# Two down projections of the layer-0 sample-side FFN as seven block products, with their weight sums made in DRAM earlier

## The chip, the cores and the metric

The kernel runs on one core of a Trainium2 chip. The core has a matrix engine (TensorE, PE in the profile; its weight loads are shown as PEld), a vector engine (VectorE, DVE), an engine for activations (ScalarE, ACT), GpSimd (POOL) and a queue engine (SyncE, SP). The first four work in order, each on its own instructions, and wait for each other and for transfers by semaphores. SP issues most of the transfers from DRAM; POOL issues those that add to what lies at the destination, and gathers. The metric is the device time of one execution in microseconds (us).

## The reference

One inference step of a decoder with two layers, width 1024, for a prompt of 1024 tokens and 8 sample tokens that share the weights, in fp32. In every layer a mixer (a gated recurrence in layer 0, stick-breaking attention in layer 1) runs beside a cross-attention into 256 memory tokens, and then comes the SwiGLU FFN, which is what the change touches:

```python
D_MODEL = 1024
D_FF = ((8 * D_MODEL + 3 * 256 - 1) // (3 * 256)) * 256

def swiglu(h, w_gu, w_down):
    gate, up = jnp.split(h @ w_gu, 2, axis=-1)
    return (jax.nn.silu(gate) * up) @ w_down
```

D_FF is 2816, which is 22 slices of 128 rows. The output of the down projection has 8 blocks of 128 columns, `m` = 0 to 7.

## The kernel before

**Tiling.** Activations lie transposed, with features on the 128 partitions and tokens along the free dimension. The tokens are split into two halves, called groups: `g = 0` has 512 prompt columns, `g = 1` has the other 512 and the 8 sample tokens, 520 columns, worked as two pieces of 260. A product in fp32 is made as three products of a faster format: a weight tile is split into a high part (a copy on ScalarE) and a rest (a subtraction on VectorE), an activation likewise, and high × high, high × rest and rest × high are added up in PSUM. `split_w` (L253) loads and splits weights, `proj` (L280) makes a projection with them, and `evac_raw` (L476) adds its result to the running output `R` in SBUF.

**FFN in steps.** The 22 slices are worked in five steps, `PARTS = [(0, 5), (5, 5), (10, 4), (14, 4), (18, 4)]` (first slice, slices). A step makes its gate and up slices, `silu(gate) * up` gives as many tiles `m`, and its down projection adds their product with the weights to `R`. Class `ffn` does this with `proj` for both groups of layer 0 (`f0`, `f1`) and for the first group of layer 1. A down step of four slices and 520 columns is 8 output blocks × 4 slices × 3 products × 2 pieces = 192 matmuls of 260 columns.

**The block form, in layer 1.** The second group of layer 1 is done by class `ffn_w`. Its steps 1, 2 and 3 have a down projection in another form, `down_w`. The weights of a step are seen as 2 × 2 blocks of 2 slices by 512 columns, the activations as 2 × 2 blocks of 2 slices by 260 columns, and the product is made of seven block products in place of eight, as Strassen's form does it. For this, four sums of weight blocks (`s1` to `s4`) are needed, and three sums of activation blocks (`ys`, made at the end of the gate and up slices). A product is 12 matmuls for each pair of output blocks; a step is 2 pairs × 7 products × 12 = 168 matmuls. The products are `product(q, j)`: `q` is one of four running sums in PSUM of which each is added to or subtracted from `R` at set points by `add` (L769, VectorE, 128 × 260), and copied with its sign turned by `minus` (L773, ScalarE). The pairs `acc[i][q]`, `i` = 0 and 1, take all eight PSUM banks, one tile of the pool "quads" for each.

**Weight sums.** They are made in DRAM, out of the weights themselves, by `summed` (L653 to L672): eight transfers for each step, four of them accumulating, each issued by POOL. So that a transfer starts at a chosen place of the program, each has a marker ahead of it: ScalarE copies one column of a tile just made (`after()`, L666; three buffers `rr`), POOL copies that (L667; one buffer `mk`), and the transfer stands behind it in POOL's order (L670 accumulating, L672 plain). `down_sums` makes them for the down weights of a layer (`dsum`, 512 KB for each transfer), `weight_sums` for the gate and up weights of layer 1 (`wsum`, 1 to 1.25 MB, five steps of eight transfers).

**The order of work.** Each part of the model is a generator, and `weave((a, na), (b, nb), ...)` runs several of them together, `na` and `nb` being how many pieces each has. What comes out is a program that a scheduler then puts into order on each engine, by its own estimate of when operands come; so weight loads and splits stand well ahead of their matmuls, and matmuls of the next projection are at times put between others. Buffers limit that: five raw weight tiles `w`, five split ones `ws`, eight tiles `a`, four tiles `c`, seven tiles `b`; in PSUM two tiles `mm` of two banks each, three of one bank `s` and one `ns`.

The stages around the change, in order: layer-0 memory attention of the first half, `a0.mem`, beside the second half's projections `a1.fq`; the output projection `o0.mm`; `o0.finish` beside `a1.v` and `a1.qm`; then layer 0's FFN for the first half; and, much later, `f1`, the second half's FFN: its steps 0 and 1 beside layer 1's attention `b0` and its steps 2, 3, 4, with `ws`, the weight sums of layer 1, beside both.

Of the kernel before, what the change touches and what calls it, by code (L numbers as in the profile page):

```python
# [9 lines left out]
F32 = mybir.dt.float32  # L10
# [8 lines left out]
P = 128  # L19
# [5 lines left out]
def tile_decoder(  # L25
# [229 lines left out]

    def split_w(W, k0, nk, m0):
        out = []
        for a in range(0, nk, 4):
            n = min(4, nk - a)
            raw = wraw.tile([P, 4, P], F32, tag="w", name=nm("w"))  # L260
            nc.sync.dma_start(
                raw[:, :n, :],
                W[(k0 + a) * P : (k0 + a + n) * P, m0 : m0 + P].rearrange("(k p) m -> p k m", p=P),
            )
            ws = wspl.tile([P, 2, 4, P], F32R, tag="ws", name=nm("ws"))
            nc.scalar.copy(ws[:, 0, :n, :], raw[:, :n, :])  # L266
            nc.vector.tensor_sub(ws[:, 1, :n, :], raw[:, :n, :], ws[:, 0, :n, :].bitcast(F32))  # L267
            for i in range(n):
                out.append((ws[:, 0, i, :], ws[:, 1, i, :]))
        return out  # L270
# [281 lines left out]

    def gate_up_w(l, f, ops, spl, raws, pair=None):
# [52 lines left out]
        mt = M(F32R)  # L606

        def put_sum(dst, d, a, b):
            nc.vector.tensor_sub(d, a, b)
            split_to((dst[:, 0], dst[:, 1]), d)  # L610

        if not pair:
            w = n if pair is None else h
            split_to((mt[:, 0, :w], mt[:, 1, :w]), sg[:, :w])
            if pair is not None:
                put_sum(mt[:, :, h:n], sg[:, :h], sg[:, h:n], sg[:, :h])
                pair.append((mt, sg))
            return mt
        m0, s0 = pair.pop()
        split_to((mt[:, 0, :n], mt[:, 1, :n]), sg[:, :n])  # L620
        y = [bpool.tile([P, 2, h], F32R, tag="b", name=nm("ys")) for _ in range(3)]
        put_sum(y[2], s0[:, h:n], s0[:, h:n], sg[:, h:n])
        put_sum(y[1], sg[:, h:n], sg[:, h:n], s0[:, :h])
        put_sum(y[0], sg[:, :h], sg[:, :h], sg[:, h:n])
        pair.extend((m0[:, :, :h], mt[:, :, :h], mt[:, :, h:n], y[0], m0[:, :, h:n], y[1], y[2]))
        return mt
# [48 lines left out]
    dsums = {}  # L675
    htok = []
# [3 lines left out]
    class ffn_w:  # L680
# [47 lines left out]
        def down_w(self, pi, f0, pairs, extra):  # L728
            l, n, h, R = self.l, NG[1], PW[1], self.R
            a11, a12, a21, a22 = down_blocks(l, f0)  # L730
            s1, s2, s3, s4 = dsums[pi]
            src = ((a11, 0), (s1, 4), (s2, 5), (a12, 1), (s3, 6), (s4, 2), (a22, 3))
            for m0 in (0, 2):
                ms = (m0, m0 + 1)
                acc = [[Q(i) for i in range(4)] for _ in ms]

                def weight(rows):
                    r = self.raws().rearrange("p k m -> p (k m)")
                    nc.sync.dma_start(r.rearrange("p (t c) -> p t c", t=2), rows[:, :, m0 * P : (m0 + 2) * P])
                    w = self.spl()  # L740
                    split_to((w[:, 0, :], w[:, 1, :]), r)
                    return w

                def slice_of(q, hf, a, first=False):
                    for i in range(2):
                        o = hf * 256 + i * P
                        for wi, (wj, xi) in enumerate(((0, 0), (0, 1), (1, 0))):
                            nc.tensor.matmul(
                                acc[i][q][:, :h], we[:, wj, o : o + P], extra[0][:, xi, a * h : (a + 1) * h],
                                start=(first and wi == 0), stop=(wi == 2), skip_group_check=True,  # L750
                            )

                def product(q, j, first=False):
                    w = weight(src[j][0])
                    for i in range(2):
                        for t in range(2):
                            x = pairs[t][src[j][1]]
                            o = t * 256 + i * P
                            for wi, (wj, xi) in enumerate(((0, 0), (0, 1), (1, 0))):
                                nc.tensor.matmul(  # L760
                                    acc[i][q][:, :h], w[:, wj, o : o + P], x[:, xi, :],
                                    start=(first and t == 0 and wi == 0), stop=(t == 1 and wi == 2),
                                    skip_group_check=True,
                                )

                def add(q, mo, a, sub=False):
                    for i, m in enumerate(ms):
                        d = R[m + mo][:, a * h : (a + 1) * h]
                        (nc.vector.tensor_sub if sub else nc.vector.tensor_add)(d, d, acc[i][q][:, :h])  # L769

                def minus(q, p):
                    for i in range(2):
                        nc.scalar.activation(acc[i][q][:, :h], acc[i][p][:, :h], AF.Copy, scale=-1.0)  # L773

                product(0, 0, True)
                minus(1, 0)
                product(3, 1, True)
                product(1, 2)
                minus(2, 1)
                product(0, 3)  # L780
                if extra:
                    tail = w_down[l][(f0 + 4) * P : (f0 + 5) * P, :].rearrange("p (o m) -> p o m", o=2)
                    we = weight(tail)
                    slice_of(0, 0, 0)
                add(3, 4, 1)
                add(0, 0, 0)
                product(1, 4)
                add(3, 0, 1, True)
                add(1, 4, 1)
                product(2, 5)  # L790
                if extra:
                    slice_of(2, 0, 1)
                add(2, 0, 1)
                product(1, 6)
                if extra:
                    slice_of(1, 1, 0)
                    slice_of(0, 1, 1, True)
                    add(0, 4, 1)
                add(1, 4, 0)
                yield  # L800

        def down(self, pi):
# [9 lines left out]
            if self.block(pi):  # L812
                yield from self.down_w(pi, f0, pairs, mids[4:])
# [29 lines left out]
    class ffn:  # L843
        def __init__(self, g, l, xt, rows=False):
            self.g, self.l, self.xt, self.rows = g, l, xt, rows
            self.R = self.acc = None

        def part(self, pi):
            g, l = self.g, self.l
# [3 lines left out]
            mids = []  # L853
            for j in range(nf):
                pg = proj(g, w_gu[l], 0, ND, (f0 + j) * P, self.xt)
                sg = silu(None, pg, g)
                pu = proj(g, w_gu[l], 0, ND, DFF + (f0 + j) * P, self.xt)
# [932 lines left out]
```

## Time and profile before

| | |
|---|---|
| runs, median | 2445.47 us (2444.11 to 2445.83, 3 runs) |
| the profiled execution | 2445.71 us |
| its span, by the profile | 2443.6 us, mean granted TensorE clock 0.998 |
| around the span | 2.1 us |
| `f1` steps 0 and 1, beside the attention | 990 to 1206.8 us |
| `f1` steps 2 to 4 | 1206.8 to 1411.3 us |
| in these, down projection of step 2 | 1250.3 to 1273.4 us |
| down projection of step 3 | 1319.3 to 1342.3 us |
| `a0.mem` with `a1.fq`, `o0.mm` | 229 to 335 us |
| the block form in layer 1, steps 2 and 3 | 2290.4 to 2310.5 and 2350.9 to 2371.0 us |

In a row of grouped instructions stand the line, the engine, the operation, output and inputs by the program's names without their numbers, and the tile; behind it the busy time and the mean of one. In a row of the timeline the first number is the start in us from the span's start and the second the length. The table of stages gives for each engine the busy time with the number of instructions, then the granted TensorE clock (1.00 is full), the mean busy share of the 16 transfer engines and their GB/s. A row of waits has the waiting engine, line and operand, what ended the wait, and then the total, how often, and the longest. In a row of the page's part on transfers the last number is the time from issue to landing.

### The profile page before, as it was taken

What the parts mean: (1) busy time and instruction counts of PE and PEld (TensorE: products, weight loads), DVE (VectorE), ACT (ScalarE), POOL (GpSimd) and SP (SyncE); (2) the same over time, 40 slices, a digit from 0 to 9 for tenths busy, and PEclk for the clock granted to TensorE, in tenths of its full rate; (3) what the DMA queues carried; (4) which work ended last, traced back from release to release, by engine and by line L of the source; (5) the groups of instructions that cost most, each with busy time, mean ns of one, the idle gap of its engine ahead of it and who ended that gap; (6) DMA issues with size and microseconds to landing.
All of it is one profiled execution on the core that took longest, in us unless ns stands there. A gap on an engine that the chain in (4) does not pass through costs nothing.

```text
span 2443.6 us, 40814 instructions
## 1 busy us (share of the span) xinstructions
PE 2403.0 (98%) x15401; PEld 2131.2 (87%) x15401; DVE 1598.5 (65%) x2785; ACT 1229.1 (50%) x2438; POOL 132.5 (5%) x201
## 2 busy tenths in 40 slices
PE   7999999999999999999999999999999999999997
PEld 6888988888877887999999989877787797999997
DVE  5777556765775576555544485777678648757885
ACT  4547544444444454555433454555454445565664
POOL 2000001200000000010111100022000000000000
PEclk9999999999999999999999999999999999999999
DMA  5353255774543446456688876544454234366651
GB/s 177 101 159 109 71 162 132 183 201 132 177 138 94 133 153 212 119 136 152 168 207 205 246 181 199 159 141 147 124 151 134 87 118 125 124 192 175 185 168 66
DMA packets 499224, 369.24 MB, mean 151 GB/s; under 512 B 19758, under 2 KB 444315, under 8 KB 499027
## 3 DMA queue, kind: packets, MB, share of 16 engines
q1 hardware_dynamic: 476114, 307.91, 42.3%
q0 software_dynamic: 22912, 58.73, 10.4%
q8 instruction: 121, 1.98, 0.3%
q14 instruction: 77, 0.62, 0.1%
HBM read 336.74 MB, written 80.15 MB: 171 GB/s over the span
## 4 chain that ended last, share of the span: by engine, by line
PE 89%; DVE 4%; DMA 2%; ACT 2%; issue 1%; SPq 0%; POOL 0%; DVEq 0%; ACTq 0%; POOLq 0%
PE mm L280 61%; PE q L581 7%; PE q L760 2%; PE q L822 2%; PE q L539 2%; PE mm L1208 2%; PE s L1058 1%; PE s L1017 1%; PE s L1391 1%; PE mm L994 1%; PE s L1566 1%; PE mm L967 1%; DMA b<-qd 1%; PE s L1605 1%; DVE ws L267 1%
## 5 line engine op out<-in xcount | busy, mean ns | idle before, releaser
L280 PE MATMUL mm<-x,ws 128*128 128x260 f32 (+1 forms) x7776 | 1329.7, 330 | 0.0
L280 PEld LDWEIGHTS mm<-x,ws 128*128 128x128 f32 x7776 | 1148.2, 188 | 143.4 <-issue 8.6
L266 ACT CAST ws<-w 128x512 fp32r<-128x512 f32 (+1 forms) x680 | 402.6, 593 | 653.1 <-PE mm L280 558.0
L267 DVE TENSOR_TENSOR ws<-w,ws 128x512 fp32r<-128x512 f32 (+1 forms) x680 | 443.4, 655 | 242.9 <-ACT ws L266 237.7
L280 PE MATMUL mm<-m,ws 128*128 128x512 f32 (+1 forms) x2112 | 392.1, 342 | 0.2 <-DVE r L476 0.2
L280 PEld LDWEIGHTS mm<-m,ws 128*128 128x128 f32 x2112 | 323.3, 188 | 47.0 <-issue 3.2
L572 DVE TENSOR_TENSOR ws<-w,ws 128x512 fp32r<-128x512 f32 x126 | 86.6, 691 | 46.4 <-ACT ws L571 43.5
L581 PE MATMUL q<-y,ws 128*128 128x260 f32 x864 | 112.7, 283 | 0.0
L581 PEld LDWEIGHTS q<-y,ws 128*128 128x128 f32 x864 | 107.3, 188 | 0.0
L476 DVE TENSOR_TENSOR r<-r,mm 128x512 f32<-128x512 f32 (+1 forms) x96 | 66.0, 688 | 57.1 <-PE mm L280 56.0
L571 ACT CAST ws<-w 128x512 fp32r<-128x512 f32 x126 | 77.8, 618 | 47.2 <-PE q L581 15.2
L320 DVE TENSOR_SCALAR t<-mm 128x512 f32<-128x512 f32 (+1 forms) x74 | 51.2, 691 | 64.3 <-PE mm L280 64.1
L858 DVE TENSOR_TENSOR t<-t,mm 128x512 f32<-128x512 f32 (+1 forms) x66 | 45.5, 689 | 67.9 <-PE mm L280 67.5
L324 DVE TENSOR_TENSOR t<-t,t 128x512 f32<-128x512 f32 (+1 forms) x66 | 45.8, 694 | 65.7 <-ACT t L323 65.7
L581 PE MATMUL q<-x,ws 128*128 128x260 f32 x648 | 86.9, 283 | 0.0
L581 PEld LDWEIGHTS q<-x,ws 128*128 128x128 f32 x648 | 81.7, 189 | 0.0
L343 DVE TENSOR_TENSOR st<-st,n 128x512 f32<-128x512 f32 (+1 forms) x98 | 67.1, 691 | 8.1 <-ACT n L342 6.6
L667 POOL COPY mk<-rr 128x1 f32<-128x1 f32 x64 | 29.3, 458 | 751.3 <-ACT rr L666 751.3
L321 ACT ACTIVATE t<-t 128x512 f32<-128x512 f32 (+1 forms) x66 | 41.9, 635 | 40.7 <-DVE t L320 36.3
L287 ACT CAST m<-t 128x512 fp32r<-128x512 f32 (+1 forms) x76 | 47.4, 623 | 25.3 <-DVE t L858 18.0
L822 PE MATMUL q<-m,ws 128*128 128x260 f32 x432 | 53.6, 284 | 0.0
L288 DVE TENSOR_TENSOR m<-t,m 128x512 fp32r<-128x512 f32 (+1 forms) x76 | 52.5, 691 | 1.2
(379 smaller groups left out, 2811.8 us busy)
## 6 DMA issues: line engine op xcount, KB each, us to landing
w<-in_w_gu SPq DMA_DIRECT2D x334, 256.0 KB, 3.2
w<-in_w_down SPq DMA_DIRECT2D x156, 256.0 KB, 3.0
w<-in_w_in_a SPq DMA_DIRECT2D x80, 256.0 KB, 3.0
wsum<-in_w_gu POOLq DMA_DIRECT2D x18, 1024.0 KB, 9.1
w<-wsum SPq DMA_DIRECT2D x72, 256.0 KB, 3.6
w<-in_w_o SPq DMA_DIRECT2D x64, 256.0 KB, 2.9
dsum<-in_w_down POOLq DMA_DIRECT2D x18, 512.0 KB, 6.5
w<-in_w_mem_kv SPq DMA_DIRECT2D x32, 256.0 KB, 3.2
```

The source lines that it names most:

```text
L266: nc.scalar.copy(ws[:, 0, :n, :], raw[:, :n, :])
L267: nc.vector.tensor_sub(ws[:, 1, :n, :], raw[:, :n, :], ws[:, 0, :n, :].bitcast(F32))
L280: nc.tensor.matmul(ps[:, a, : PW[g]], wt, xt[k][:, xi, o : o + PW[g]], start=(k == 0 and wi == 0), stop=(k == nk - 1 and wi == 2),)
L288: nc.vector.tensor_sub(dst[1], src, dst[0].bitcast(F32))
L320: nc.vector.tensor_scalar(sv(x, g), pv(ps, g), -44.0, None, op0=ALU.max)
L343: nc.vector.tensor_add(acc[:, :n], acc[:, :n], t[:, :n])
L476: nc.vector.tensor_add(dst, dst, pv(ps, g))
L539: nc.tensor.matmul(pp[a][:, :h], wt, xt[k][:, xi, a * h : (a + 1) * h], start=(k == 0 and wi == 0), stop=(k == ND - 1 and wi == 2),)
L571: nc.scalar.copy(w[:, 0, :], src)
L572: nc.vector.tensor_sub(w[:, 1, :], src, w[:, 0, :].bitcast(F32))
L581: nc.tensor.matmul(ps[:, :h], w[:, wj, k * P : (k + 1) * P], x[:, xi, :], start=(first and k == 0 and wi == 0), stop=(k == 3 and wi == 2), ...
L822: nc.tensor.matmul(pp[a][:, :h], wt, mids[k][:, xi, a * h : (a + 1) * h], start=(k == 0 and wi == 0), stop=(k == nf - 1 and wi == 2),)
```

## The change

The down projections of steps 2 and 3 of `f1` (layer 0, second group) use the block form. `down_w` becomes a function of its own that gets its PSUM tiles, buffers and a hook from the caller; it now yields twice for each pair of output blocks. The function `paired`, which makes the activation sums, is taken out of `gate_up_w`, so that `ffn` can use it. In `ffn` the four running sums of a pair have other PSUM tiles: `q = 0` and `q = 3` a bank each (`s`, or `ns` for the last), `q = 1` and `q = 2` the two banks of one `mm` tile. The steps' order becomes: gate and up of step 2, the first slice of step 3, down of step 2, the rest of step 3, the first slice of step 4, down of step 3, the rest of step 4, its down.

The weight sums of these two steps are 16 transfers, put beside `a0.mem` with `a1.fq` (7), `o0.mm` (5) and `o0.finish` with `a1.v` and `a1.qm` (4); their markers read a split weight tile (`now`). Of the 40 steps of layer 1's weight sums, 21 in place of 16 now stand beside the attention and 19 in place of 24 beside steps 2 to 4.

```diff
+            now[0] = ws[:, 0, 0, 0:1].bitcast(F32)
...
+    def paired(sg, pair):
...
-            dsums[i] = t
+            dsums[l, i] = t
...
+    def down_w(l, pi, R, pairs, extra, raws, spl, banks, each):
...
+            acc = [banks(i) for i in range(2)]
...
+            add(0, 0, 0)
+            yield
+            product(1, 4)
+            add(3, 0, 1, True)
+            add(1, 4, 1)
+            product(2, 5)
...
+            add(2, 0, 1)
+            product(1, 6)
...
+            add(1, 4, 0)
+            each(ms)
+            yield
...
+        def spl(self):
+            self.n += 1
+            if self.n % 8 in (1, 4, 6):
+                return cpool.tile([P, 2, 512], F32R, tag="c", name=nm("ws"))
+            return wspl.tile([P, 2, 512], F32R, tag="ws", name=nm("ws"))
+
+        def raws(self):
+            self.r += 1
+            if self.r % 2:
+                if not self.half:
+                    t = apool.tile([P, 2, 4, P], F32, tag="a", name=nm("w"))
+                    self.half = [t[:, 0], t[:, 1]]
+                return self.half.pop(0)
+            return wraw.tile([P, 4, P], F32, tag="w", name=nm("w"))
...
+                sg = silu(N() if block else None, pg, g)
...
+                if block:
+                    mids.append(paired(sg, pairs[j // 2]))
...
+                def four(i):
+                    two = mmp.tile([P, 2, 512], F32, tag="mm", name=nm("mm"))
+                    return [S(), two[:, 0, :], two[:, 1, :], NS() if i else S()]
...
+                yield from down_w(l, pi, self.R, pairs, mids[4:], self.raws, self.spl, four, each)
+                return
...
-    weave((a0.mem(), 8), (a1.fq(), 8))
+    ds = down_sums(0, (2, 3), lambda: now[0])
+    weave((a0.mem(), 8), (a1.fq(), 8), (islice(ds, 7), 8))
     o0 = out_proj(0, 0, M)
-    drain(o0.mm(a0.xo))
-    weave((o0.finish(), 17), (chain(a1.v(), a1.qm(A)), 8))
+    weave((o0.mm(a0.xo), 8), (islice(ds, 5), 5))
+    weave((o0.finish(), 17), (chain(a1.v(), a1.qm(A)), 8), (ds, 4))
...
-    f1 = ffn(1, 0, o1.x)
+    f1 = ffn(1, 0, o1.x, (2, 3))
     ws = weight_sums(1, range(5), lambda: f1.now, 4)
-    weave((chain(b0.sb(), b0.mem()), 24), (chain(f1.part(0), f1.part(1)), 18), (islice(ws, 16), 17))
-    weave((chain(f1.part(2), f1.part(3), f1.part(4)), 24), (ws, 24))
+    weave((chain(b0.sb(), b0.mem()), 24), (chain(f1.part(0), f1.part(1)), 18), (islice(ws, 21), 22))
+    lagged = chain(
+        f1.gate_up(2), f1.gate_up(3, 0, 1), f1.down(2), f1.gate_up(3, 1), f1.gate_up(4, 0, 1), f1.down(3),
+        f1.gate_up(4, 1), f1.down(4),
+    )
+    weave((lagged, 24), (ws, 19))
```

On TensorE, at the down projection of step 2, an output block stood before as a run over the four slices `m`, three products and two pieces each, in one `mm` tile; the next block follows with the other tile:

```order
L280 MATMUL mm_12366<-m_11947,ws_12363 128x260 x6
L280 MATMUL mm_12366<-m_12085,ws_12363 128x260 x6
L280 MATMUL mm_12366<-m_12219,ws_12363 128x260 x6
L280 MATMUL mm_12366<-m_12353,ws_12363 128x260 x6
L280 MATMUL mm_12397<-m_11947,ws_12394 128x260 x6
L280 MATMUL mm_12397<-m_12085,ws_12394 128x260 x6
```

Now, in the first pair of output blocks of that step, the rows from the end of product(1, 2) on read as follows. `mm_12640` and `mm_12643` hold q1 and q2 of `i` = 0 and 1, `s_12790` is q0 of the next pair, and rows of `m_12201` with `mm` are product(1, 4), of `ys_12204` product(2, 5):

```order
L715 MATMUL mm_12643<-ys_12489,ws_12728 128x260 x3
L715 MATMUL s_12790<-m_12064,ws_12797 128x260
L715 MATMUL mm_12640<-m_12201,ws_12749 128x260 x3
L715 MATMUL mm_12640<-m_12484,ws_12749 128x260 x3
L715 MATMUL s_12790<-m_12064,ws_12797 128x260 x2
L715 MATMUL mm_12643<-m_12201,ws_12749 128x260 x3
L715 MATMUL mm_12643<-m_12484,ws_12749 128x260 x3
L715 MATMUL s_12790<-m_12347,ws_12797 128x260 x2
L715 MATMUL mm_12640<-ys_12204,ws_12767 128x260 x3
L715 MATMUL mm_12640<-ys_12487,ws_12767 128x260 x3
```

Single matmuls of the next pair's product(0, 0) have moved between the products of the first pair. In the second pair of each step the products stand one behind the other.

On VectorE, in the second pair of step 2, the sums (L724) stand between weight splits (L269) of the gate and up weights that come next. The first row is an add of q3, then come those of q0 (`s`), and those of q1 and q2 (`mm`):

```order
L724 TENSOR_TENSOR r_10159<-r_10159,ns_12794 128x260 x2
L269 TENSOR_TENSOR ws_12946<-w_12944,ws_12946 128x512
L724 TENSOR_TENSOR r_10159<-r_10159,s_12790 128x260
L269 TENSOR_TENSOR ws_13007<-w_13005,ws_13007 128x512
L724 TENSOR_TENSOR r_10159<-r_10159,s_12793 128x260
L269 TENSOR_TENSOR ws_13012<-w_13010,ws_13012 128x512
L724 TENSOR_TENSOR r_10159<-r_10159,mm_12789 128x260
L724 TENSOR_TENSOR r_10159<-r_10159,mm_12792 128x260
L724 TENSOR_TENSOR r_10159<-r_10159,mm_12789 128x260
L724 TENSOR_TENSOR r_10159<-r_10159,mm_12792 128x260
L269 TENSOR_TENSOR ws_13082<-w_13080,ws_13082 128x512
L724 TENSOR_TENSOR r_10159<-r_10159,mm_12789 128x260
```

Where before one sum of 520 columns followed each output block, six sums of 260 columns for each `i` now follow the products of a pair.

More of the change, by code (lines that the diff above doesn't have):

```diff
@@ L605, in gate_up_w @@
         nc.vector.tensor_mul(sg[:, h:n], sg[:, h:n], gt[:, h:n])
[L606 to L626, printed above, removed]
+        return paired(sg, pair)
     sums = {}
@@ L726, in gate_up @@
                 yield
[L728 to L800, printed above, removed]
@@ L812, in down @@
             if self.block(pi):
-                yield from self.down_w(pi, f0, pairs, mids[4:])
+                yield from down_w(
+                    l, pi, self.R, pairs, mids[4:], self.raws, self.spl, lambda i: [Q(q) for q in range(4)], lambda ms: None
+                )
                 return
@@ L852, in part @@
             last = pi == len(PARTS) - 1
[L853 to L857, printed above, removed]
-                nc.vector.tensor_mul(sv(sg, g), sv(sg, g), pv(pu, g))
-                mt = M(F32R)
-                split_to((mt[:, 0, :n], mt[:, 1, :n]), sg[:, :n])
-                mids.append(mt)
-                self.now = sg[:, 0:1]
-                yield
+            mids, pairs = self.mids.pop(pi)
             if pi == 0:
```

110 lines of the change are left out of this document (102 added, 8 removed).

## The prediction

> **What bounds the kernel now.** I read the page's busy times first, then its chain of waits, then a table of busy time by stage, and last the rows of single engines inside the stages that the change touches.
>
> ```profile
> span 2443.6 us, 40814 instructions
> PE 2403.0 (98%) x15401; PEld 2131.2 (87%) x15401; DVE 1598.5 (65%) x2785; ACT 1229.1 (50%) x2438; POOL 132.5 (5%) x201
> PE 89%; DVE 4%; DMA 2%; ACT 2%; issue 1%; SPq 0%; POOL 0%; DVEq 0%; ACTq 0%; POOLq 0%
> PE mm L280 61%; PE q L581 7%; PE q L760 2%; PE q L822 2%; PE q L539 2%; PE mm L1208 2%; PE s L1058 1%; PE s L1017 1%; PE s L1391 1%; PE mm L994 1%; PE s L1566 1%; PE mm L967 1%; DMA b<-qd 1%; PE s L1605 1%; DVE ws L267 1%
> ```
>
> TensorE is busy for 98% of the span and carries 89% of the chain, 61% of it by the plain projections of L280. A matmul taken out therefore shortens the kernel by its own time, unless TensorE then waits. The stages, in order of time (before the layer-0 second half; its steps 0 and 1 beside attention; its steps 2 to 4; layer 1's two block downs), read:
>
> ```profile
> core 0: us, PE busy (x) PEld busy (x) DVE busy (x) ACT busy (x) POOL busy (x), PEclk, DMA share, GB/s
> 1250.30:1273.40 23.10, 23.10 (x195) 23.10 (x194) 11.64 (x17) 6.27 (x13) 4.21 (x7) 1.00 0.90 214
> 1206.80:1411.30 204.50, 204.50 (x1709) 204.46 (x1708) 101.92 (x149) 82.31 (x150) 31.33 (x47) 1.00 0.83 213
> 2290.40:2310.50 20.10, 20.10 (x170) 20.10 (x169) 18.54 (x42) 11.90 (x24) 0.00 (x0) 1.00 0.66 187
> 2350.90:2371.00 20.10, 20.10 (x171) 20.10 (x170) 18.32 (x41) 11.73 (x23) 0.00 (x0) 1.00 0.64 184
> 990.00:1206.80 216.80, 215.11 (x1699) 207.64 (x1699) 120.08 (x219) 111.63 (x247) 22.84 (x34) 1.00 0.56 141
> 229.00:335.00 106.00, 105.88 (x659) 95.20 (x658) 58.46 (x114) 60.07 (x133) 0.00 (x0) 1.00 0.30 91
> ```
>
> From 1206.8 to 1411.3 us TensorE has no gap at all (204.50 of 204.50), at the full clock, with VectorE busy for half of the time and ScalarE for 40%. This is where the two steps stand.
>
> **The matmuls removed.** The two plain down projections are runs of 192 matmuls of 260 columns; the block form already runs in layer 1 on steps of the same size (four slices), as 168 matmuls of 260 columns.
>
> ```profile
> 1250.32 23.20 PE L280 MATMUL mm<-m,ws 128*128 128x260 f32 x192
> 1273.36 46.08 PE L280 MATMUL mm<-x,ws 128*128 128x260 f32 x384
> 1319.28 23.21 PE L280 MATMUL mm<-m,ws 128*128 128x260 f32 x192
> 1342.33 46.08 PE L280 MATMUL mm<-x,ws 128*128 128x260 f32 x384
> ```
>
> The next group's start less this one's: 1273.36 − 1250.32 = 23.04, and 1342.33 − 1319.28 = 23.05, together 46.09 us. The same two steps as block products, from the chain of waits in layer 1:
>
> ```profile
> 2290.42 20.13 PE q L760 x168
> 2350.92 20.06 PE q L760 x168
> ```
>
> These are 40.19 us, with the waits that the form has there. The term is 46.09 − 40.19 = −5.90 us. By pitch it is 2 × 24 matmuls × 0.120 us (23.04 / 192) = −5.76; I take the whole steps. The Trainium skill (TensorE: Matmul & The Clock Gate, "Wait — 56ns, not 53.3ns?") gives a warm matmul one column per cycle at 2.4 GHz and 2.5 ns on top, which for 260 columns is an estimate of 111 ns, and 48 of them 5.3 us. The trace's pitch of 120 ns is longer, so the measurement decides.
>
> **What the copied form does not bring along.** In layer 1 each of the four running sums of a pair has a PSUM tile of its own. Here q1 and q2 are the two banks of one mm tile, and a wait is made for a whole tile. So product(2,5) must wait until VectorE's add(1,4,1) has read q1, product(1,6) until add(2,0,1) has read q2, and the projection after the step until add(1,4,0) has read q1. What that costs is seen from the sums of layer 1:
>
> ```profile
> L769 DVE TENSOR_TENSOR r<-r,q x76: 414/420/428, 2215.9 to 2371.2; 128x260 f32<-128x260 f32 x76
> 2304.05 1.29 DVE L572 TENSOR_TENSOR ws<-w,ws 128x512 fp32r<-128x512 f32 x2
> 2305.53 0.42 DVE L769 TENSOR_TENSOR r<-r,q 128x260 f32<-128x260 f32 x1 [0.20 <-PE q L760]
> 2304.62 1.60 PE L760 MATMUL q<-m,ws 128*128 128x260 f32 x12
> L760 PEldq EVENT_SEMAPHORE  x3: 51/51/51, 2215.4 to 2352.6; - x3
> ```
>
> A product is 12 matmuls, six for each of the two tiles i. The sixth of the run that starts at 2304.62 starts at 2304.62 + 5 × 0.12 = 5.22, and ends, by its 0.28 us (1.60 − 11 × 0.12), near 5.50; the add starts at 5.53. So the path "last matmul's start, add, next matmul" takes about 0.31 + 0.42 + 0.05 (TensorE's own wait instruction) = 0.78 us. Between that matmul and the one that writes the same mm tile stand the six matmuls of the other i, so the next start would come 7 × 0.12 = 0.84 us after it. An add that finds VectorE free is thus hidden by 0.06 us, and one that stands behind a weight split (two take 1.29, so 0.65 each) need not be.
>
> The order of VectorE shows where that is so. In the first column pair of each step TensorE has matmuls of the next pair's product(0,0) between (1,4), (2,5) and (1,6), five in one step and four in the other, up to 0.6 us of further cover; I count nothing there. In the second pair nothing is left to put between. In the first step's second pair VectorE has: add of q0 for i = 0, split, add of q0 for i = 1, split, and then the adds of q1. Counted from the start of the last q0 matmul of i = 0, with 0.36 us from one add's start to the next's: the add starts at 0.31, the split takes the time to 1.32, the second add to 1.68, the second split to 2.33, and q1's add runs from there to 2.75, so product(2,5) may start at 2.80 where TensorE is ready at 19 × 0.12 = 2.28. That is 0.5 us late if no split could start earlier, and 0 if both did; I take 0.35, nearer to late, since no split passes an add on VectorE. A split between add(2,0,1) and add(1,4,0) delays the projection behind the step by about 0.2, in both steps; in the second step no split stands ahead of q1's adds. With two wait instructions of 0.05 more than layer 1 has: 0.35 + 0.2 + 0.2 + 0.1 = 0.85 us. The ends: nothing (all hidden), and a split ahead of each of the six waits in the two uncovered pairs, 12 × 0.59 (0.65 - 0.06) = 7.1 us.
>
> **VectorE and ScalarE.** A down step goes from 8 sums of 520 columns and 8 splits (17 VectorE instructions with one of its neighbours, 11.64 us, in the first of the stage rows) to 24 sums of 260 columns and 14 splits, as layer 1's 18.54 us (x42); the gate and up steps get the paired sums and their splits, about six more instructions of 0.42 to 0.65 for each of four pairs. In sum VectorE gets 2 × 6.9 + 4 × 3.1 + 1.7 (one more ScalarE-paced group) = 28 us, so 130 of 199. ScalarE gets 2 × 5.6. Both stay beside TensorE; if the cover goes, it goes where a split is late, which is the term above.
>
> **Weight sums moved.** Sixteen steps of the sums for these two down projections come new, at 229 to 371 us: a copy on ScalarE of one column, a copy on POOL, and a DMA of 512 KB on POOL's queue. The nearest rows are layer 1's:
>
> ```profile
> L666 ACT COPY rr<-t x36: 184/187/191, 400.7 to 1389.7; 128x1 f32<-128x1 f32 x36
> dsum<-in_w_down POOLq DMA_DIRECT2D x18, 512.0 KB, 6.5
> POOL wsum L670 <- DMA wsum<-wsum: 26.1, 6, 5.8
> POOL wsum L672 <- DMA wsum<-in_w_gu: 25.1, 4, 8.0
> PE s L1593 <- DVE b L1587: 5.0, 8, 2.3
> ```
>
> Of the early stage, the page loads and the weight loads:
>
> ```profile
> 248.28 6.09 PE L280 MATMUL mm<-x,ws 128*128 128x260 f32 x48
> 256.18 6.09 PE L280 MATMUL mm<-x,ws 128*128 128x260 f32 x48
> 1581.02 1.26 POOL L1144 DMA_INDIRECT c<-in_cache_sb_k,pidx  x1 [157.24 <-DVE sc L1099]
> w<-in_w_gu SPq DMA_DIRECT2D x334, 256.0 KB, 3.2
> ```
>
> The copies cost ScalarE 16 × 0.19 = 3.0 us of a stage in which it is busy for 60 of 106; each also waits up to 0.65 us for the split that it reads. POOL is idle there (0.00), and DMA has a share of 0.30. One step falls to about one projection, and these follow each other at 7.9 us (256.18 − 248.28), longer than a landing's 6.5, so POOL keeps up. Cost nothing, hidden by a load queue that runs five buffers ahead; without that cover, 16 × 0.65 = 10 us of ScalarE delay at most. Of the gate and up sums five more steps, and 14 of the down step's loads (into tiles of the attention), move into the stage at 990 to 1206.8, where DMA has a share of 0.56 and 141 GB/s. TensorE loses 1.7 us there in all, part of it on L1593, so a late transfer has room. SP issues 28 loads in place of 16 for the two steps; the first of them stand behind loads that wait for an attention tile, and what is queued behind those (weights for a later step) has time. On POOL's queue the page loads of the sample attention now stand behind the sums; the first pages are read shortly before 1581 us, when the next page load gets its buffer. I take 0 for all of it, between 0 and +6.6 (two weight loads at 6.5 in place of 3.2 us).
>
> **The sum.** 2445.71 (profiled execution: span 2443.6 and 2.1 around it) − 5.90 + 0.85 = 2440.66; the runs' median, 2445.47, is 0.24 lower than the profiled execution, so about 2440.4 for a run.
>
> **The rivals.** B, the shared bank pair costs in part or in full: waits between 1.4 and 7.1 us, so 2441 to 2446.7; for it speaks VectorE at 18.54 of 20.10 us in layer 1's down, against it that VectorE's order has a split ahead of q1's and q2's adds in few places. C, the gain is lost elsewhere: in the attention stage the transfers grow from 141 to about 185 GB/s (five steps of 1.3 MB, read and written, and 3.5 MB of loads), and a weight load that lands like a sum, after 6.5 in place of 3.2 us, costs 3.3 us where no buffer runs ahead: once or twice, 2443.7 to 2447.0. Against it: the next stage runs at 213 GB/s with no TensorE gap. D, the other side: the markers. A step's ScalarE copy needs one of three tokens, freed by POOL, and POOL stands in each accumulating DMA's wait (26.1 and 25.1 us above). Eight steps hold about five landings that follow one another; with 21 steps over 216.8 us, eight take 83, so it decides from landings of 16.5 us on, and the casts for TensorE then stand behind the token. At 17.5 us it costs 5 groups × (87.5 − 82.5) = 25 us, less 5.1: about 2465. E, slower too: TensorE's clock drops in the two steps, because PSUM tiles turn round more often and it pauses between groups. At half clock the two steps take 40.19 us more: about 2480. The two layer-1 rows above have PEclk 1.00 with all eight banks in the same turn, so this has little. The Trainium skill (TensorE: Matmul & The Clock Gate, "A second HAM failure mode: psum-queue depth-cycling") describes such an oscillation between half and full clock from PSUM cycling; in layer 1 the trace disagrees.
>
> **How the numbers follow.** A, the forecast, 0.56 (2439.6 to 2441.2); B 0.27; C 0.08; D 0.06; E 0.03. Of no change I speak within 0.2%, 4.9 us, about what a measurement of this kernel can tell: faster is below 2440.6. Of A 0.50 lies below, and 0.02 of C, so faster 0.52; same 0.06 + 0.25 + 0.06 + 0.02 = 0.39; slower 0.09 (D 0.04, E 0.03, B with further delays 0.02). The range, 2439.2 to 2447.0, reaches from the full 5.90 with nothing lost (2439.6, and 0.4 for the spread of the runs) to B's and C's upper ends.
>
> **What would show it.** In the profile after, two runs of 168 matmuls from L715 of 20.1 to 20.6 us each in the chain of waits; TensorE waits on L715 and on the projection behind it for the sums of L724 of 0.2 to 0.5 us, in the second pairs; VectorE near 130 us in the stage; no TensorE wait between 229 and 371 us; POOL's waits for DMA under 9 us each. Waits on L715 in the first pairs, or more than 1.2 us in all, mean B; a wait for ScalarE or a DMA between 990 and 1207 us means C; ScalarE's L673 idle before a POOL copy means D; PEclk under 1.00 means E.

## The result, and the profile after

The changed kernel takes 2455.79 us (median of 7 runs, 2448.53 to 2460.05); the kernel before, run beside it, 2445.74 us (7 runs, 2444.11 to 2447.26). The ratio is 1.0037, with a 95% interval of 1.0023 to 1.0051: slower by 10 us between the medians and 9 by the ratio, where about 5 us faster was forecast, and with a spread three to four times as wide. The profiled execution took 2456.64 us with a span of 2454.9 us.

The page of the kernel after, the lines that answer to those of before:

```profile
span 2454.9 us, 40938 instructions
PE 2403.9 (98%) x15353; PEld 2130.0 (87%) x15353; DVE 1619.9 (66%) x2861; ACT 1245.5 (51%) x2498; POOL 151.4 (6%) x233
PE 85%; DVE 6%; DMA 4%; ACT 2%; issue 2%; SPq 0%; POOL 0%; DVEq 0%; ACTq 0%; POOLq 0%
```

TensorE executes 48 matmuls fewer (15353 for 15401), as planned, and yet is as busy; in the chain that ended last its share falls from 89 to 85%, and transfers and VectorE take 4 and 6%. The table of stages, with the two block steps in rows 1 and 3 and the gate and up slices behind each:

```profile
1259.47:1282.43 22.96, 20.91 (x170) 20.27 (x168) 18.94 (x42) 11.66 (x29) 4.42 (x8) 1.00 0.92 219
1282.43:1329.58 47.15, 46.28 (x385) 46.10 (x385) 24.73 (x45) 21.20 (x40) 2.27 (x4) 1.00 0.59 156
1329.58:1361.89 32.31, 22.55 (x171) 21.50 (x169) 18.05 (x39) 10.92 (x26) 13.17 (x16) 0.95 0.95 258
1361.89:1397.97 36.08, 36.08 (x289) 36.08 (x290) 14.72 (x22) 14.03 (x24) 2.84 (x4) 0.95 0.70 187
```

The down of step 2 takes 22.96 us, as long as the plain form did (23.04), and the down of step 3 takes 32.31. So the gain is gone in step 2, and 9 us are lost in step 3 (32.31 for 23.05). The waits of TensorE say for whom:

```profile
PE mm L715 <- DVE r L724: 8.1, 5, 4.6
PE mm L283 <- DVE ws L269: 3.2, 1, 3.2
PE mm L283 <- DVE n L889: 0.9, 1, 0.9
PE mm L283 <- DVE r L724: 0.5, 1, 0.5
```

L715 are the block products, L724 the sums into `R`, L269 the split of a weight for a gate or up projection, L283 the projections; the 3.2 us are the projection behind step 3, which waits for a late weight of its own. The end of step 3 on the timeline (start, length, engine, and in brackets the idle time before with what ended it) shows where the longest ones come from:

```profile
1349.47 1.70 PE L715 MATMUL mm<-m,ws 128*128 128x260 f32 x12 [1.20 <-DVE r L724]
...
1354.01 0.62 ACT L268 CAST ws<-w 128x512 fp32r<-128x512 f32 x1 [5.90 <-DMA w<-in_w_gu]
1354.66 0.69 DVE L269 TENSOR_TENSOR ws<-w,ws 128x512 fp32r<-128x512 f32 x1 [4.91 <-ACT ws L268]
1355.27 0.75 DVE L724 TENSOR_TENSOR r<-r,mm 128x260 f32<-128x260 f32 x2
1355.74 2.97 PE L715 MATMUL mm<-ys,ws 128*128 128x260 f32 x12 [4.58 <-DVE r L724]
...
1360.15 0.62 ACT L268 CAST ws<-w 128x512 fp32r<-128x512 f32 x1 [5.53 <-DMA w<-in_w_gu]
1360.80 0.69 DVE L269 TENSOR_TENSOR ws<-w,ws 128x512 fp32r<-128x512 f32 x1 [4.78 <-ACT ws L268]
```

It is a chain of four links. A gate weight lands late; ScalarE's cast waits for it; VectorE's split waits for the cast; and the sum `add(2, 0, 1)`, whose operand has long been there, stands behind that split in VectorE's order. The product that waits for the sum, product(1, 6), does not even use the bank that the sum reads; it writes the other bank of the same `mm` tile. The profile's chain of waits puts two numbers on the first link, a piece in each step:

```profile
1268.65 11.95 DMA w<-in_w_gu
...
1338.01 22.05 DMA w<-in_w_gu
```

11.95 and 22.05 us from issue to landing, where the loads issued in the same step of the kernel before took 3.7 (median) and 6.9 at most. In step 2 the late load cost TensorE little: there its waits for sums are 1.13, 0.38 and 0.55 us, and only the last stands behind that load. The long waits, 4.58 and 3.17 us, are in step 3. The transfers of that plain step and of the two block steps (rows of the queues; q0 is POOL's, q1 SP's; the last number is the share of the 16 engines' time), first before, then after:

```profile
q0 software_dynamic: 1216, 2.95, 58.6%
q1 hardware_dynamic: 3963, 1.96, 31.1%
w<-in_w_gu SPq DMA_DIRECT2D x8, 256.0 KB, 3.7
```

```profile
q0 software_dynamic: 1429, 3.83, 69.8%
q1 hardware_dynamic: 2344, 1.17, 21.3%
...
q0 software_dynamic: 2320, 6.71, 76.0%
q1 hardware_dynamic: 3213, 1.60, 18.9%
c<-in_cache_sb_k,pidx POOLq DMA_INDIRECT x8, 6.3
```

SP's weight loads moved at 1.96 MB / 23.1 us = 85 GB/s before, and at 1.17 / 22.96 = 51 and 1.60 / 32.31 = 50 GB/s after. POOL's queue holds the rest: four weight sums start within the down of step 2 and four in that of step 3, where three had started in each plain down, and in step 3 the eight page gathers of the sample attention come on top. In the kernel before, these eight ran at 936 to 941 and at 1202 to 1210 us, ahead of the steps.

### The profile page after: what moved, and what is told of

Its sections match the earlier page's. It is cut to its first block, busy times and chain, and to the rows that moved or that the text cites. A ratio compares the mean times of both kernels' runs of the same rounds, so it can differ in the third digit from the quotient of the medians.

```text
span 2454.9 us, 40938 instructions
## 1 busy us (share of the span) xinstructions
PE 2403.9 (98%) x15353; PEld 2130.0 (87%) x15353; DVE 1619.9 (66%) x2861; ACT 1245.5 (51%) x2498; POOL 151.4 (6%) x233
## 4 chain that ended last, share of the span: by engine, by line
PE 85%; DVE 6%; DMA 4%; ACT 2%; issue 2%; SPq 0%; POOL 0%; DVEq 0%; ACTq 0%; POOLq 0%
PE mm L283 57%; PE q L608 7%; PE q L715 2%; PE q L833 2%; PE q L542 2%; PE mm L1254 2%; DMA w<-in_w_gu 1%; PE s L1104 1%; PE s L1063 1%; DMA b<-qd 1%; PE s L1437 1%; PE mm L1040 1%; PE mm L1013 1%; DVE ws L269 1%; PE s L1612 1%
## 5 line engine op out<-in xcount | busy, mean ns | idle before, releaser
L283 PE MATMUL mm<-x,ws 128*128 128x260 f32 (+1 forms) x7776 | 1331.7, 330 | 4.7 <-DVE ws L269 3.2
L283 PEld LDWEIGHTS mm<-x,ws 128*128 128x128 f32 x7776 | 1149.9, 188 | 148.9 <-issue 9.6
L268 ACT CAST ws<-w 128x512 fp32r<-128x512 f32 (+1 forms) x664 | 392.6, 592 | 614.6 <-PE mm L283 495.8
L269 DVE TENSOR_TENSOR ws<-w,ws 128x512 fp32r<-128x512 f32 (+1 forms) x664 | 432.6, 655 | 248.7 <-ACT ws L268 241.8
L283 PE MATMUL mm<-m,ws 128*128 128x512 f32 (+1 forms) x1728 | 346.6, 356 | 0.1
L283 PEld LDWEIGHTS mm<-m,ws 128*128 128x128 f32 x1728 | 277.9, 189 | 47.0 <-issue 3.1
L599 DVE TENSOR_TENSOR ws<-w,ws 128x512 fp32r<-128x512 f32 x126 | 86.5, 691 | 48.2 <-ACT ws L598 44.6
L674 POOL COPY mk<-rr 128x1 f32<-128x1 f32 x80 | 37.2, 465 | 1193.4 <-ACT rr L673 1193.2
L598 ACT CAST ws<-w 128x512 fp32r<-128x512 f32 x126 | 77.8, 618 | 49.2 <-PE q L608 15.8
L479 DVE TENSOR_TENSOR r<-r,mm 128x512 f32<-128x512 f32 (+1 forms) x80 | 54.9, 686 | 36.9 <-PE mm L283 35.9
L327 DVE TENSOR_TENSOR t<-t,t 128x512 f32<-128x512 f32 (+1 forms) x58 | 40.2, 693 | 54.7 <-ACT t L326 54.7
L889 DVE TENSOR_TENSOR t<-t,mm 128x512 f32<-128x512 f32 (+1 forms) x58 | 39.9, 689 | 53.3 <-PE mm L283 52.8
L291 DVE TENSOR_TENSOR ws<-w,ws 128x512 fp32r<-128x512 f32 x72 | 48.9, 687 | 20.8 <-ACT ws L290 20.4
L290 ACT CAST ws<-w 128x512 fp32r<-128x512 f32 x72 | 43.7, 616 | 33.7 <-DMA w<-dsum 11.6
```

The costliest lines, as they stand in the source:

```text
L283: nc.tensor.matmul(ps[:, a, : PW[g]], wt, xt[k][:, xi, o : o + PW[g]], start=(k == 0 and wi == 0), stop=(k == nk - 1 and wi == 2),)
L290: nc.scalar.copy(dst[0], src)
L479: nc.vector.tensor_add(dst, dst, pv(ps, g))
L598: nc.scalar.copy(w[:, 0, :], src)
L599: nc.vector.tensor_sub(w[:, 1, :], src, w[:, 0, :].bitcast(F32))
```

## The experiments

Two links could be cut: what makes the loads late (the weight sums, or the page gathers, beside the block steps), and what hands a late load on to TensorE (the shared `mm` tile). A third question was whether the rest of the change (early sums, sums beside the attention, new order) costs anything. All times are medians of ten runs (four for the kernel with the weight sums behind the FFN), beside the kernel before on the same chip; the times of steps are each from one profiled execution.

**Only the rest of the change.** The block form is switched off.

```diff
-    f1 = ffn(1, 0, o1.x, (2, 3))
+    f1 = ffn(1, 0, o1.x, ())
```

> Everything of the change but the block products: the two down steps run the plain way again (192 matmuls each), with the new order of the steps, the 16 early sums (made, read by nobody) and the weight sums at 21 and 19. If the loss lies in the block steps alone, the time is that of the kernel before, 2444.5 to 2447. If the early sums, or the sums moved beside the attention, cost TensorE something, it is above 2448.

2445.71 us against 2445.72, ratio 1.0 (0.999 to 1.0009). The early sums, the five sums moved beside the attention and the order of the steps cost nothing that can be told; both plain downs take 22.99 us in it (1262.94 to 1285.93 and 1331.85 to 1354.84), with three weight sums starting in each. The loss needs the block form.

**The banks by running sum.** One `mm` tile holds q1 of both `i`, the other q2.

```diff
-                    two = mmp.tile([P, 2, 512], F32, tag="mm", name=nm("mm"))
-                    return [S(), two[:, 0, :], two[:, 1, :], NS() if i else S()]
+                    if not i:
+                        twos[:] = [mmp.tile([P, 2, 512], F32, tag="mm", name=nm("mm")) for _ in range(2)]
+                    return [S(), twos[0][:, i, :], twos[1][:, i, :], NS() if i else S()]
```

> The two mm tiles of a pair are cut the other way: one holds q1 of both i, the other q2 of both i, so that a product never waits for the sum of the other running total. If the shared tile is the cause, the waits of TensorE on L715 for VectorE's sums (8.1 us in five) go, the two steps fall from 22.96 and 32.31 us to about 20.3 each, and the time to about 2443. If late weight loads are the cause (a cast on ScalarE that waits for its load holds VectorE's splits and sums behind it), the wait moves to the projection behind the step, which needs the late weights itself: the small waits of 0.4 to 1.2 us go, at most 3 us are won, and the time is 2451 to 2455.

2445.32 us, ratio 0.9998 (0.9988 to 1.0008): some 10 us less than the change, so the time lies between the two expectations. Step 2 falls to 21.29 us. Step 3 is still 26.28 us, and its longest wait has only changed its owner:

```profile
1344.68 0.62 ACT L268 CAST ws<-w 128x512 fp32r<-128x512 f32 x1 [2.56 <-DMA w<-in_w_gu]
1345.20 0.37 ACT L728 ACTIVATE mm<-mm 128x260 f32<-128x260 f32 x1
...
1345.62 2.97 PE L715 MATMUL mm<-ys,ws 128*128 128x260 f32 x12 [2.46 <-ACT mm L728]
...
1352.47 34.70 PE L283 MATMUL mm<-x,ws 128*128 128x260 f32 x288 [1.00 <-DVE r L724]
```

L728 is the sign-turned copy on ScalarE: now it is this copy that stands behind a cast that waits for its load. Step 2 falls although the sums and a late load are still there (a cast waits 2.9 us for it, 3.1 in the change), so what it lost was the shared tile's. The shared tile was one way on to TensorE, and not the only one.

**The page gathers held back** until the FFN of the second half is done.

```diff
+    tok = small([P, 1], tag="rr")
+    nc.scalar.copy(tok, f1.now)
+    held[0] = nc.gpsimd.tensor_copy(small([P, 1], tag="mk", bufs=1), tok).ins
...
-                nc.gpsimd.indirect_dma_start(
+                with tc.issue_after(held[0]):
+                    nc.gpsimd.indirect_dma_start(
```

> The eight page gathers of the sample attention, 2 MB, are held on POOL's queue until the second half's FFN is done. If they crowd the weight loads out in step 3, its 32.31 us fall to 22 to 25 and the time to 2446 to 2449; step 2 stays at 23. If the weight sums crowd them out, or the shared tile is the cause, step 3 stays above 29 us and the time at 2452 to 2456.

2446.48 us, ratio 1.0002 (0.9993 to 1.0012). Step 3 falls from 32.31 to 25.28 us, step 2 stays at 23.1, close to what was expected of gathers that crowd the loads out (22 to 25). Without them the wait at product(1, 6) is 1.63 us in place of 4.58.

**The weight sums behind the FFN.** The 19 transfers that stood beside steps 2 to 4 stand beside the output projection, the norms, the key and value projection and the query heads that follow.

```diff
-    weave((lagged, 24), (ws, 19))
+    drain(lagged)
+    at[0] = lambda: now[0]
...
-    drain(kv_proj(1, xk1))
+    weave((kv_proj(1, xk1), 8), (islice(ws, 6), 6))
```

> The 19 weight-sum transfers (1 MB each) that stood beside steps 2 to 4 stand behind them instead, beside the projections and norms that follow. If these transfers, of which up to four start within 13 us, hold the weight loads up, both steps fall to 20.3 to 21.5 us and the time to 2441 to 2444, as long as the later stages hide them. If the page gathers or the shared tile are the cause, step 3 keeps more than 5 us of its excess: 2447 or above.

The steps do much as expected: 21.36 and 21.67 us (20.3 to 21.5), though page gathers still run in step 3, and no cast waits for a gate or up weight. The time does not, for it hung on the later stages: the kernel takes 2469.96 us, ratio 1.0097 (1.0081 to 1.0114): the stages behind cannot hide the transfers. Four of the waits that TensorE got there, by far the longest for norms:

```profile
PE ns L335 <- DVE st L346: 11.2, 2, 9.4
PE mm L283 <- ACT a L1503: 3.9, 1, 3.9
PE s L1612 <- DMA a<-ksc: 3.2, 1, 3.2
PE s L1582 <- ACT t L1577: 2.9, 2, 1.9
```

So it is the sums that make the loads late, with the gathers making it worse while they are there; but a later place is no place for them.

**Two cuts together, banks and gathers:** the two edits above.

> Both of the single edits that won about 10 us: mm tiles by running sum, and the page gathers held back. If each took away a different link (the shared tile hands a late cast on to TensorE, the gathers make the cast late), together they leave step 2 at 21.3 us and step 3 at 21 to 23, and the time is 2440 to 2443. If they removed the same 10 us, no more than 1 us is won over the better of the two: 2444.5 to 2446.

2445.28 us, ratio 0.9996 (0.9986 to 1.0005): the same as either edit alone, as the second theory had it. Step 2 takes 21.3 us and step 3 25.0; in step 3 one load still takes 11.53 us to land, and ScalarE's sign-turned copies wait behind its cast. The first theory, that each edit cuts a link of its own and the two add up, is ruled out; neither takes the sums away from the steps.

**The weight sums with the gate and up slices only.** The same transfers, the same stage; no marker is put into a block step.

```diff
-    weave((lagged, 24), (ws, 19))
+    weave((chain(f1.gate_up(2), f1.gate_up(3, 0, 1)), 5), (islice(ws, 7), 7))
+    drain(f1.down(2))
+    weave((chain(f1.gate_up(3, 1), f1.gate_up(4, 0, 1)), 4), (islice(ws, 6), 6))
+    drain(f1.down(3))
+    weave((chain(f1.gate_up(4, 1), f1.down(4)), 7), (ws, 6))
```

> The same 19 weight-sum transfers, but none started by a marker inside a block down step: 7 with the gate and up slices before the down of step 2, 6 with those before the down of step 3, 6 behind it. The page gathers still fall into step 3. If it is the transfers that run during the two down steps that hold the weight loads up, step 2 falls to about 21.4 us (as with all 19 moved behind), step 3 to 22 to 25 with the page gathers still there, and the time to 2442 to 2446. If the amount moved between 1215 and 1420 us counts and not its place, waits of TensorE for late loads show up in the gate and up slices, and the time is above 2448.

2441.46 us, ratio 0.9984 (0.9974 to 0.9994). This edit alone turns the loss into a gain of some 4 us. Step 2, though, is 22.69 us where about 21.4 was expected: with no cast waiting for a load there, the shared tile's waits of 1.11, 0.38 and 0.29 us are still there. The stages of this kernel, in the order of the table above:

```profile
1258.45:1281.14 22.69, 20.91 (x170) 20.29 (x168) 18.95 (x42) 11.27 (x26) 1.42 (x2) 1.00 0.88 186
1281.14:1327.17 46.03, 46.03 (x385) 46.03 (x385) 24.77 (x45) 22.19 (x44) 5.25 (x10) 1.00 0.58 156
1327.17:1349.39 22.22, 20.96 (x170) 20.31 (x168) 18.12 (x39) 10.22 (x23) 7.04 (x9) 1.00 1.04 299
1349.39:1383.93 34.54, 34.53 (x289) 34.54 (x289) 14.68 (x22) 14.03 (x24) 5.18 (x6) 1.00 0.72 164
```

Step 3 moves more per second than in the change (299 GB/s for 258), page gathers included, and no cast waits for a gate or up weight. One sum starts in each step here, and in step 2 SP's loads are back at 2.10 MB in 22.69 us, 93 GB/s. In step 3 two more sums had started just ahead of it, at 1324.68 and 1325.89 us. The queues' rows, for 1336 to 1352 us of the change and then for step 3 of this kernel in two parts, 1327.17 to 1338 and 1338 to 1349.39, show what they do:

```profile
q0 software_dynamic: 1307, 3.95, 89.9%
q1 hardware_dynamic: 999, 0.50, 12.3%
...
q0 software_dynamic: 949, 2.75, 93.9%
q1 hardware_dynamic: 614, 0.31, 11.6%
...
q1 hardware_dynamic: 3308, 1.64, 51.5%
q0 software_dynamic: 574, 1.91, 49.7%
```

Beside sums SP's queue moves 0.50 MB in 16 us, 31 GB/s, in the change (where gathers run too), and 0.31 MB in 10.83 us, 29 GB/s, here too. In the second part of the step, when the sum started at 1325.89 has landed (after 12.3 us) and seven of the gathers run, it moves 1.64 MB in 11.39 us, 144 GB/s. So SP's queue is slow beside sums in both kernels. Here that is over before the casts want the next weights; in the change three sums start at 1334.51, 1335.49 and 1337.42, just as SP issues three of those loads (1336.13 to 1338.37).

**The last two cuts on top of that.** Banks by running sum with the sums at the gate and up slices; the held gathers with them; and all three.

> mm tiles by running sum and weight sums only with the gate and up slices; the page gathers fall into step 3 again. If the gathers cost little once the weight sums are out of the step, step 3 stays at 20.5 to 21.2 us (20.56 without them) and the time at 2439.5 to 2441.5; if they crowd weight loads out by themselves, step 3 is above 22 us. Set against the run with the shared tile as the change has it (22.69 and 22.22 us), step 2 tells what the shared tile costs by itself: I expect 1.5 us there.

> The shared tile as the change has it, with the page gathers held back and the weight sums only with the gate and up slices. If what is left in the steps then is the shared tile alone, step 2 stays at 22.7 us and step 3 at 21.7 to 22.2, each wait of TensorE on L715 is for a sum of VectorE and none is longer than 1.2 us; the time is 2441 to 2443. If the gathers caused the waits of step 3 in the run with them, step 3 falls below 21 us.

> All three: mm tiles by running sum, page gathers held back, weight sums only with the gate and up slices. If late loads and the shared tile are the whole loss, both steps come to 20.2 to 20.8 us, TensorE waits nowhere on L715 for more than 0.3 us, and the time is 5 to 6 us below the kernel before: 2439.5 to 2441. If something else is left, a step stays above 21.5 us.

| kernel | us | ratio to before (95%) | step 2 | step 3 |
|---|---|---|---|---|
| sums at the gate and up slices | 2441.46 | 0.9984 (0.9974 to 0.9994) | 22.69 | 22.22 |
| and gathers held | 2442.53 | 0.9982 (0.9973 to 0.9992) | 22.73 | 21.80 |
| and banks by running sum | 2439.00 | 0.9972 (0.9962 to 0.9981) | 21.22 | 20.36 |
| all three | 2440.11 | 0.9978 (0.9968 to 0.9988) | 21.19 | 20.56 |

With the sums out of the way the gathers cost nothing that can be told (20.36 us with them, 20.56 without; with the shared tile 22.22 and 21.80), and the shared tile costs 22.69 − 21.22 = 1.47 us in step 2 and 22.22 − 20.36 = 1.86 in step 3. The four intervals overlap, so what the tile costs rests on the times of the steps. With all three edits step 2 was expected at 20.2 to 20.8 us and is 21.19: something is left there that none of them removes. The kernel with banks by running sum and sums at the gate and up slices beats both the kernel before and the change. Its steps follow the gate and up slices with hardly a gap:

```profile
1259.06 2.34 PE L715 MATMUL s<-m,ws 128*128 128x260 f32 x18
...
1280.28 46.08 PE L283 MATMUL mm<-x,ws 128*128 128x260 f32 x384
1326.19 2.33 PE L715 MATMUL s<-m,ws 128*128 128x260 f32 x18
...
1346.55 34.61 PE L283 MATMUL mm<-x,ws 128*128 128x260 f32 x288
```

## Why the prediction was wrong

**The matmuls removed, −5.90: right.** 48 matmuls are gone, at the old pitch. In the best kernel (banks by running sum, sums at the gate and up slices) the two steps take 21.22 + 20.36 = 41.58 us against 45.98 plain (22.99 twice): 4.4 us. Most of what is missing to 5.90 is step 2's 21.22 us, where layer 1's took 20.13. Nearly all of the difference is in the first pair of output blocks (11.09 us for 10.04; the second pair 10.13 for 10.09); one wait there is for a sign-turned copy, 0.36 us, and the rest is not explained.

**The shared bank pair, +0.85: the mechanism right, the size not.** It measured 1.47 + 1.86 = 3.3 us where loads are on time. What mis-sized this term is "I count nothing there", for the first pair of each step. There is the longest of these waits, 1.1 us in step 2, the first pair's product(2, 5). The cover of single matmuls from the next pair did not help, since one of them could run and the rest stood behind. The rows of the kernel after, first pair of step 2, show splits between the sums exactly as in the second pair:

```profile
1266.33 0.42 DVE L724 TENSOR_TENSOR r<-r,s 128x260 f32<-128x260 f32 x1
1266.67 0.69 DVE L291 TENSOR_TENSOR ws<-w,ws 128x512 fp32r<-128x512 f32 x1
1267.27 0.42 DVE L724 TENSOR_TENSOR r<-r,s 128x260 f32<-128x260 f32 x1
1267.61 0.42 DVE L724 TENSOR_TENSOR r<-r,mm 128x260 f32<-128x260 f32 x1
1268.08 0.98 PE L715 MATMUL mm<-m,ws 128*128 128x260 f32 x6 [1.13 <-DVE r L724]
```

The second pair's wait at the same place was 0.38 us and the projection's 0.3 to 0.55, near the 0.35 and 0.2 that were taken. The price hangs on how far VectorE has come: with the weight sums behind the FFN the same tile left 21.36 and 21.67 us; there the first sum of q1 in step 2 started 0.90 us after product(1, 4) had, and not 2.33 us as with the sums at the gate and up slices, and the 1.1 us wait was gone. What puts VectorE ahead there was not tried. (In the words behind the second order listing ahead of the prediction, the rows begin at the end of product(1, 4), those of `m_12201` with `mm` are product(2, 5), and those of `ys_12204` product(1, 6).)

**Weight sums moved, 0: right for the two places that were looked at, and yet the step that failed.** Between 229 and 371 us, and between 990 and 1206.8 us, TensorE is as busy as before (141.52 us after and 141.84 before in the first, 215.19 and 215.11 in the second). But "I take 0 for all of it" left out the place where the sums that did not move met the new loads. Five sums left the stage of steps 2 to 4, but in the down steps themselves there were four in place of three, and the block form asks for 14 loads in 20 us in place of 8 in 23, with the gate weights of the next slices behind them. The page gathers, dismissed as wanted only after 1580 us, were looked at for when they are needed and not for where they now run: in step 3, since the tiles they load into now serve as weight buffers before (the first of them waits for a matmul of L715). That a late split reaches TensorE through the bank pair was in the prediction, but at a split's length of 0.65 us, and not with a load behind the split that lands after 22. So where the sum had 0, moving the weight sums to the gate and up slices took 10.1 us from step 3 (32.31 to 22.22).

**Rivals.** B was true, and worth 3.3 us of the 16.8 between the change and the best kernel where loads are on time; where they are late, the shared tile was the way by which most of the delay reached TensorE. C was the nearest in kind (a weight load that lands late), but in the wrong stage, and with a landing of 6.5 us taken from a sum, where 12 and 22 were to come. D did not happen: the markers' ScalarE copies waited for nothing longer than 1.2 us, on VectorE; the sums did their harm as transfers. E happened on a small scale and as a consequence: after the long waits the clock is at half for some 3 us. From the table of stages of the kernel after, the wait, the product behind it, and the same for the next wait:

```profile
1352.00:1355.70 3.70, 0.00 (x0) 0.00 (x0) 1.04 (x3) 0.62 (x1) 0.57 (x1) 0.96 1.06 276
1355.70:1358.70 3.00, 2.96 (x12) 2.67 (x12) 0.32 (x1) 0.00 (x0) 0.00 (x0) 0.50 1.13 212
1358.70:1361.80 3.10, 0.01 (x1) 0.00 (x0) 1.00 (x3) 0.62 (x1) 1.90 (x2) 0.98 1.07 299
1361.80:1364.40 2.60, 2.51 (x13) 2.52 (x14) 0.37 (x2) 0.00 (x0) 0.00 (x0) 0.58 1.15 336
```

Twelve matmuls take 2.97 us in place of 1.60, and the 288 that follow the step 36.08 in place of 34.54: 2.9 us in all that the waits cost beside themselves.

**The sum told again by the runs.** From the best kernel to the change: step 2 22.96 − 21.22 = 1.7, step 3 32.31 − 20.36 = 12.0, the slow clock behind it 1.5, the gate and up slices between the steps 47.15 − 45.91 = 1.2. That is 16.4 us of the 16.8 between the medians, or of the 17.5 between the spans of the two profiles that the steps are read from. The bytes of a step do not decide: in step 3 of the run with the sums at the gate and up slices POOL's queue moved 4.65 MB in 71.2% of the engines' time and TensorE waited for no load, where 3.83 MB and 69.8% in step 2 of the change made one take 11.95 us. What fits both is whether SP's queue is slow (31 GB/s in the change, 29 here) just when weights are wanted. What stays open is whether the number of sums or their coming close together makes that stretch long, since no run moved them within a step, and what in a weight sum slows SP's queue.

## What to carry to other kernels

When a stage's matmuls are made fewer, ask what its loads per microsecond become and which transfers already run beside it: here the form with an eighth less work needs 14 loads where 8 did, and transfers that were free beside the old form cost 14 us beside the new one (2455.79 − 2441.46), while in the slices between they are free again. A wait travels by engine order, from a late load over a cast and a split to a sum that needs neither; two running sums in one PSUM tile gave it the last link. Laying them out so that a product waits for its own running sum alone won 3.3 us with the loads on time, but with late loads the wait found another way. And a prefetch that is harmless where it is wanted may move: look for where it runs after the change, not for when it is needed.

## What the runs showed of the hardware that was not expected

TensorE's granted clock fell to 0.50 after a wait of 4.6 us in the change, and already after waits of 2.5 us (banks by running sum) and 2.1 us (banks and gathers), and stayed there for about 3 us. After the first two, 12 matmuls took 2.97 us; after the third the first dozen took 2.08 and the next 2.80. After 1.63 us (gathers held back) it did not fall (12 matmuls in 1.71). The Trainium skill (TensorE: Matmul & The Clock Gate, "HAM oscillation — how this bites in real kernels") gives waits above about 3.4 us as those that bite; here shorter ones did, so the measurement decides. The same section's picture, a wait for a transfer followed by a cold group of matmuls, fits the rows, though here the transfer's delay comes to TensorE by way of a sum or a sign-turned copy.

SP's loads fell to 50 GB/s over the block steps beside POOL's sums, and to 31 within step 3, and a load of 256 KB took up to 22.05 us to land, six times the 3.7 us of the plain step; in the stretch with seven page gathers SP's queue kept 144 GB/s. The Trainium skill (DMA: Bandwidth & Descriptors, "SWDGE vs HWDGE vs iDMA") says that each engine takes turns between its queues; that does not by itself say why POOL's queue with sums in it takes 93.9% of the engines' time and leaves SP's 11.6%, and with seven gathers 49.7% and 51.5%, and no run here shows it.
